# Half-block products in a two-layer decoder trunk: block sums kept in three half-size buffers and loaded three columns ahead

## The chip, the cores and the metric

The kernel runs on one core of a Trainium2 chip. The metric is the device time of one execution in microseconds (us). The profile uses short names for the engines: PE (matrix multiplication, with its weight loads shown as PEld), DVE (the vector engine), ACT (the scalar engine), POOL (the general engine, which here also issues DMAs) and SP (which only issues DMAs).

## What is computed

Two layers work on 512 positions of width 1024. The first mixes positions with a convolution module, the second with sparse attention, and each is followed by the same feed-forward network:

```python
def swiglu_ffn(h, w_in, w_out):
    gate, up = jnp.split(h @ w_in, 2, axis=-1)
    return (jax.nn.silu(gate) * up) @ w_out

for i in range(DEPTH):
    h = rmsnorm(x, norm_mix[i])
    x = x + mixer_i(h)
    h = rmsnorm(x, norm_ffn[i])
    x = x + swiglu_ffn(h, ffn_w_in[i], ffn_w_out[i])
```

The hidden width is 2816, which is 22 columns of 128. Only the products with `w_in` of 17 of these 22 columns, in both layers, are touched by the change.

## The kernel before

Data stand transposed: 128 features lie on the partitions, 512 positions along the rows. The products with the large weights are made exact enough by splitting each operand into a rounded high part and a low remainder. ACT writes the high part, DVE subtracts it from the original to get the low part, and PE adds up three products: high by high, high by low, low by high.

The feed-forward function `ffn` (line 636) makes the first five hidden columns (`NREG`) with ordinary products, two output tiles for each (gate and up). The other 17 (`NST`) are made by `pair` (line 791), once for each column. A column's weights are seen as four blocks of 512 elements: gate and up, each with a first and a second half of the inner dimension. The activations are seen as four blocks too (two halves of the inner dimension, two halves of the 512 positions, `H` = 256 each). With sums and differences of the blocks, seven products are enough instead of eight. So a column takes seven calls of `product` (line 759), each of twelve matmuls with a 128x256 moving operand: 84 matmuls.

The activation side is prepared once for each layer: `operand(c)` (line 695) is called for the four pieces of the inner dimension while the ordinary columns are still computed. DVE scales the input into `z`, POOL makes the differences `t1` to `t4`, and ACT and DVE split everything into `bh` and `bl`.

The weight side is prepared anew for each column n, in these steps:

- `s_load(n)`: SP loads one weight block into `raw[n]` (two buffers).
- `s_pre(n)`: POOL issues a DMA that puts two weight blocks into blocks 0 and 2 of the tile `S[n]` (four blocks of 512, two buffers).
- `s_acc(n)`: POOL issues an accumulating DMA, which adds a third block to both of them in place.
- `s_add(n)`: POOL adds the gate weights, which are the tile `wr`, to make block 1 from block 0 (line 741) and block 3 from block 1 (line 742).
- `s_g1(n)` and `s_g2(n)`: `s_part` splits blocks 0 and 1 into the parts `ga`, and blocks 2 and 3 into the parts `gb`. ACT copies 1024 elements (line 748), then DVE subtracts 1024 elements (line 749). The parts of `raw[n]` are `gc`. Each of these part tiles has one buffer, so the parts of column n+1 wait until PE has read those of column n.

Within `pair(n)` PE's order is written out by hand. I number its products:

- P0 uses the gate tile's own split `w1`, which `w_hi` (ACT, line 191) and `w_lo` (DVE, line 200) make ahead. The trace has them right behind P4 of an earlier pair.
- P1 uses the first half of `ga`.
- P2 (in `tail`) uses `gc` of the column before and ends that column.
- P3 uses the second half of `ga`.
- P4 uses `w1` again.
- P5 uses the second half of `gb`.
- P6 uses the first half of `gb`.

Small steps on ACT and DVE pick up the results: `copied` makes `c1`, `c5` and `c2` on ACT (line 770), DVE adds the two halves of `g` (lines 821 and 825), ACT applies silu to `g` (line 826), `t22` adds on DVE (line 789), and `post` multiplies on DVE (lines 782 and 783). P2 cannot begin before `t22` of the column before, because both touch the same bank.

Nearly all of these instructions carry `keep_in_program_order` (written `pe`), so each engine runs them in the order of the program text. For POOL this gives, in pair n: both adds of column n+1, the DMA issue of `s_pre(n+2)`, and then the DMA issue of `s_acc(n+2)`. An engine waits in place: whatever stands behind a waiting instruction on POOL waits too. `w_hi`, `w_lo` and the loads of `wr` are not pinned; the compiler's scheduler may move them.

Before the first pair the loop over the ordinary columns issues, at its fourth `operand`: two `s_load`, then on POOL `s_pre(0)`, `s_acc(0)`, `s_pre(1)`, `s_add(0)`, `s_acc(1)`.

Of the kernel before, what the change touches and what calls it, by code (L numbers as in the profile page):

```python
# [10 lines left out]
F32 = mybir.dt.float32  # L11
F32R = mybir.dt.float32r
BF16 = mybir.dt.bfloat16
I32 = mybir.dt.int32
AF = mybir.ActivationFunctionType
ALU = mybir.AluOpType
# [3 lines left out]
P = 128  # L20
T = 512
# [66 lines left out]
NST = NF - NREG  # L88
NB = 7
# [17 lines left out]
def trunk(ctx: ExitStack, tc: tile.TileContext, A, out):  # L107
    nc = tc.nc
# [8 lines left out]
    def nm(s):  # L117
        cnt[0] += 1
        return f"{s}_{cnt[0]}"
# [32 lines left out]
    for z in QV_ORDER:  # L152
        if z < 8:
            add("nw_q", z, 1024)
        else:
            w = VW[z - 8]
# [46 lines left out]
    def next_w(ahead=True):  # L203

        i = state["next"]
        w_hi(i)
        w_lo(i)
        state["next"] += 1
        if ahead and i + 1 < state["end"]:
            w_hi(i + 1)  # L210
        for k in range(i, min(i + 4, state["end"])):
            w_dma(k)
        return split[i]
# [25 lines left out]
    def v(col, n=1):  # L239
        return vec[:, col:col + n]  # L240
# [395 lines left out]
    def ffn(acc, gnext, layer):  # L636
# [7 lines left out]
        H = T // 2  # L644
        pe = tc.keep_in_program_order
        with ExitStack() as cx:
# [6 lines left out]
            sw = sx.enter_context(tc.tile_pool(name="sw", bufs=1, side="right", reuse_waits="tile"))  # L653
# [39 lines left out]
            bh, bl = [], []  # L693

            def operand(c):
                z = sw.tile([P, 4 * T], F32, tag="S", bufs=2, name=nm("z"))
                for i in range(2):
                    nc.vector.scalar_tensor_tensor(z[:, i * T:(i + 1) * T], x[c + 4 * i], v(gcol + c + 4 * i), R,
                                                   ALU.mult, ALU.mult)
                b11, b12, b21, b22, t1, t2, t3, t4 = (z[:, i * H:(i + 1) * H] for i in range(8))  # L700
                gp = nc.gpsimd
                gp.tensor_tensor(t1, b11, b12, ALU.subtract)
                gp.tensor_tensor(t3, b22, b12, ALU.subtract)
                gp.tensor_tensor(t2, t1, b22, ALU.add)
                gp.tensor_tensor(t4, t2, b21, ALU.subtract)
                gp.tensor_scalar(t2, t2, -1.0, None, ALU.mult)
                h_ = sb.tile([P, NB * H], F32R, tag=f"bh{c}", name=nm("bh"))
                l_ = sb.tile([P, NB * H], F32R, tag=f"bl{c}", name=nm("bl"))
                for d, e in ((slice(0, H), slice(0, H)), (slice(H, NB * H), slice(2 * H, 8 * H))):
                    nc.scalar.activation(h_[:, d], z[:, e], AF.Copy)  # L710
                    nc.vector.tensor_tensor(l_[:, d], z[:, e], h_[:, d], ALU.subtract)
                bh.append(h_)
                bl.append(l_)


            W, S, raw, part = {}, {}, {}, {}

            def s_load(n):
                if n >= NST:
                    return  # L720
                W[n] = A["fw_x"][layer * NST + n]
                raw[n] = sw.tile([P, T], F32, tag="r22", bufs=2, name=nm("r22"))
                nc.sync.dma_start(raw[n], W[n][:, :T])

            def odd(n):
                return S[n].rearrange("p (a c b) -> p a c b", a=2, c=2)[:, :, 0]

            def s_pre(n):
                if n >= NST:
                    return  # L730
                S[n] = sw.tile([P, 4 * T], F32, tag="S", bufs=2, name=nm("S"))
                pe(nc.gpsimd.dma_start(odd(n), W[n][:, :2 * T].rearrange("p (a b) -> p a b", a=2)))  # L732

            def s_acc(n):
                if n < NST:
                    pe(nc.gpsimd.dma_start(odd(n), W[n][:, None, 2 * T:].to_broadcast([P, 2, T]), accum_op=ALU.add))

            def s_add(n):
                if n < NST:
                    w = raws[u0 + n]  # L740
                    pe(nc.gpsimd.tensor_tensor(S[n][:, T:2 * T], S[n][:, :T], w[:, :T], ALU.add))  # L741
                    pe(nc.gpsimd.tensor_tensor(S[n][:, 3 * T:], S[n][:, T:2 * T], w[:, T:2 * T], ALU.add))  # L742

            def s_part(n, key, of, cols):

                h_ = sw.tile([P, cols], F32R, tag=key + "h", name=nm("sh"))
                l_ = sw.tile([P, cols], F32R, tag=key + "l", name=nm("sl"))
                pe(nc.scalar.activation(h_, of, AF.Copy))  # L748
                pe(nc.vector.tensor_tensor(l_, of, h_, ALU.subtract))  # L749
                part[n, key] = (h_, l_)  # L750

            def s_g1(n):
                if n < NST:
                    s_part(n, "ga", S[n][:, :2 * T], 2 * T)

            def s_g2(n):
                s_part(n, "gb", S[n][:, 2 * T:], 2 * T)

            def product(ps, w, i, b, first, last):
                wh, wl = w  # L760
                for c in range(4):
                    k = slice(i * T + c * P, i * T + (c + 1) * P)
                    t = slice(b * H, (b + 1) * H)
                    for q, (p_, m_) in enumerate(((wh, bh), (wh, bl), (wl, bh))):
                        pe(nc.tensor.matmul(ps[:, :H], p_[:, k], m_[c][:, t], start=first and c == 0 and q == 0,  # L765
                                            stop=last and c == 3 and q == 2, skip_group_check=True))

            def copied(ps, tag):
                t = ft.tile([P, H], F32, tag=tag, name=nm(tag))
                pe(nc.scalar.activation(t, ps[:, :H], AF.Copy))  # L770
                return t

            def bank():
                return pm.tile([P, T], F32, tag="pm", name=nm("st"))
# [9 lines left out]

                return post

            def t22(q):
                q["t"] = ft.tile([P, H], F32, tag="t22", name=nm("t22"))
                pe(nc.vector.tensor_tensor(q["t"], q["a"][:, :H], q["c5"], ALU.add))

            def pair(n, prev):
                q = dict(n=n, a=bank())
                last = n == NST - 1
                w1 = next_w(False)
                product(q["a"], w1, 0, 0, True, True)
                if prev:
                    t22(prev)
                s_g2(n)
                s_add(n + 1)
                s_load(n + 2)  # L800
                s_pre(n + 2)
                q["d"] = bank()
                product(q["d"], part[n, "ga"], 0, 3, True, True)
                c1 = copied(q["a"], "c1")
                post = tail(prev) if prev else None
                q["c5"] = copied(q["d"], "c5")
                if post:
                    post()
                w_hi(state["next"])
                w_lo()  # L810
                product(q["a"], part[n, "ga"], 1, 4, False, True)
                s_part(n, "gc", raw[n], T)
                b = bank()
                product(b, w1, 1, 1, True, True)
                c2 = copied(q["a"], "c2")
                s_g1(n + 1)
                if last:
                    product(q["a"], part[n, "gb"], 0, 5, False, True)
                product(q["d"], part[n, "gb"], 1, 2, False, True)
                g = q["g"] = ft.tile([P, T], F32, tag="g", name=nm("g"))  # L820
                pe(nc.vector.tensor_tensor(g[:, :H], b[:, :H], c1, ALU.add))
                s_acc(n + 2)
                if not last:
                    product(q["a"], part[n, "gb"], 0, 5, False, True)
                pe(nc.vector.tensor_tensor(g[:, H:], q["d"][:, :H], c2, ALU.add))
                pe(nc.scalar.activation(g, g, AF.Silu))
                return q

            act(0, pss[0], pss[1])
# [2 lines left out]
            for f in range(2, NREG):  # L832
                mids = []
                for z in range(2):
                    mids.append(proj_tile(pm, "pm"))
                    i = 2 * (f - 2) + z
                    if i < 4:
                        operand(i)
                    if i == 3:
                        s_load(0)  # L840
                        s_load(1)
                        s_pre(0)
                        s_acc(0)
                        s_pre(1)
                        s_add(0)
                        s_acc(1)
                act(f, *mids)
            hx[0].close()
            yx = ExitStack()
# [4 lines left out]
            q = None  # L854
            for n in range(NST):
                q = pair(n, q)
            t22(q)
            tail(q)()
            sx.close()
            fo = cx.enter_context(tc.tile_pool(name="fo", bufs=1, side="right", reuse_waits="tile"))  # L860
# [1 line left out]
            for m in range(NK):  # L862
                ps = pm.tile([P, T], F32, tag="pm", name=nm("fo"))
                for b, n in ((0, 8), (8, 8), (16, 6)):
                    wh, wl = next_w()
                    for k in range(n):
                        c = slice(k * P, (k + 1) * P)
# [11 lines left out]
                else:  # L879
                    n = OUT_N if m == NK - 1 else T  # L880
# [846 lines left out]
```

## Time and profile before

| what | value |
|---|---|
| time, median of 3 runs | 1408.66 us (1407.66 to 1409.84) |
| time of the profiled execution | 1403.82 us |
| its span in the trace | 1401.8 us |
| mean granted clock of PE | 0.962 |
| PE busy | 1280.7 us (91%), 8015 matmuls |
| DVE busy | 769.2 us (55%) |
| ACT busy | 561.8 us (40%) |
| POOL busy | 385.5 us (27%) |

The span runs from the first to the last instruction that the profiler saw; the execution's own time is 2 us longer. Busy shares are means over stages that differ much. PE's busy time also grows when its clock is low, because each matmul then takes longer, so a high share does not say that PE does useful work all the time. The chain of work that ended last names, step by step backwards, what released each piece of work; it is the view that tells which engine or transfer sets the time in a stage.

### The profile page before, as it was taken

Reading aid. Unit: us, or ns where it says so; the run is one execution under the profiler, and the core shown is the slowest. Engines: PE = TensorE matmul, PEld = TensorE weight load, DVE = VectorE, ACT = ScalarE, POOL = GpSimd, SP = SyncE. Lnnn points to the kernel's source line nnn. Section 1 sums busy time; section 2 is a strip of 40 time slices with the busy share of each in tenths; the row PEclk is TensorE's granted clock in tenths of the full one; section 3 lists DMA queues with packets and bytes.
Section 4 is the critical chain, followed back from the end, with each engine's and each line's share of the span. In section 5 each row is a group of like instructions: output and inputs, shape, how many; then the busy total and the mean of one; then the engine's idle time right before and its main releaser. Section 6 shows DMA issues by size and latency. Waiting matters only on the chain.

```text
span 1401.8 us, 20567 instructions
## 1 busy us (share of the span) xinstructions
PE 1280.7 (91%) x8015; PEld 1073.5 (77%) x8015; DVE 769.2 (55%) x1355; ACT 561.8 (40%) x970; POOL 385.5 (27%) x435
## 2 busy tenths in 40 slices
PE   8999899978887899999998999999998888879998
PEld 6887687877886878888777766668777788777887
DVE  6993778544443462335687787634763444346222
ACT  5222544433343342223453677743443434334111
POOL 2011036332323201131332556522543333230000
PEclk9999999999899899999999999999999899989999
DMA  8668232554454412344255010003255554541331
GB/s 322 216 228 242 60 114 76 158 140 118 129 136 118 125 59 92 98 118 118 91 137 146 17 46 9 16 31 106 84 149 128 136 128 136 128 124 64 110 105 57
DMA packets 82114, 161.61 MB, mean 115 GB/s; under 512 B 36064, under 2 KB 36960, under 8 KB 80480
## 3 DMA queue, kind: packets, MB, share of 16 engines
q1 hardware_dynamic: 65808, 108.54, 25.4%
q0 software_dynamic: 16208, 51.75, 14.2%
q8 instruction: 63, 1.03, 0.3%
q14 instruction: 35, 0.29, 0.1%
HBM read 146.73 MB, written 5.28 MB: 108 GB/s over the span
## 4 chain that ended last, share of the span: by engine, by line
PE 47%; DMA 18%; issue 13%; POOL 10%; DVE 9%; ACT 2%; SPq 2%; DVEq 0%; POOLq 0%; ACTq 0%
DMA S<-fw_x 16%; PE fo L253 6%; PE fo L252 6%; PE fo L251 6%; PE pp L253 5%; PE pp L251 5%; PE pp L252 5%; POOL S L741 3%; PE O L1468 3%; POOL S L742 3%; PE cpe L462 2%; PE st L765 2%; POOL S L732 2%; PE pv L1303 1%; DVE Pm L1414 1%
## 5 line engine op out<-in xcount | busy, mean ns | idle before, releaser
L200 DVE TENSOR_TENSOR wl<-wr,wh 128x1024 fp32r<-128x1024 f32 (+3 forms) x158 | 189.5, 1200 | 200.3 <-ACT wh L191 193.0
L191 ACT ACTIVATE wh<-wr 128x1024 fp32r<-128x1024 f32 (+3 forms) x158 | 160.4, 1015 | 328.5 <-PE fo L252 145.0
L765 PE MATMUL st<-bh,sh 128*128 128x256 f32 x680 | 213.9, 315 | 53.7 <-ACT sh L748 48.8
L765 PE MATMUL st<-bh,sl 128*128 128x256 f32 x680 | 212.8, 313 | 27.0 <-DVE sl L749 27.0
L765 PE MATMUL st<-bl,sh 128*128 128x256 f32 x680 | 208.5, 307 | 0.0
L765 PEld LDWEIGHTS st<-bh,sh 128*128 128x128 f32 x680 | 147.1, 216 | 62.2 <-ACT sh L748 55.0
L749 DVE TENSOR_TENSOR sl<-S,sh 128x1024 fp32r<-128x1024 f32 x68 | 85.8, 1264 | 188.4 <-ACT sh L748 188.4
L765 PEld LDWEIGHTS st<-bh,sl 128*128 128x128 f32 x680 | 147.6, 217 | 34.2 <-DVE sl L749 34.2
L253 PE MATMUL pp<-hh,wl 128*128 128x512 f32 x416 | 164.8, 399 | 3.9 <-DVE wl L200 3.9
L251 PE MATMUL pp<-hh,wh 128*128 128x512 f32 x416 | 165.3, 400 | 2.9 <-DVE gr L409 1.9
L252 PE MATMUL pp<-hl,wh 128*128 128x512 f32 x416 | 165.3, 398 | 0.1
L765 PEld LDWEIGHTS st<-bl,sh 128*128 128x128 f32 x680 | 147.6, 217 | 0.1
L252 PE MATMUL fo<-al,wh 128*128 128x512 f32 x352 | 139.8, 397 | 2.6 <-DVE al L670 2.6
L253 PE MATMUL fo<-ah,wl 128*128 128x512 f32 x352 | 139.4, 397 | 1.5 <-DVE wl L200 1.5
L251 PE MATMUL fo<-ah,wh 128*128 128x512 f32 x352 | 139.8, 397 | 1.0 <-ACT wh L191 1.0
L748 ACT ACTIVATE sh<-S 128x1024 fp32r<-128x1024 f32 x68 | 71.4, 1050 | 143.3 <-POOL S L741 142.7
L253 PEld LDWEIGHTS pp<-hh,wl 128*128 128x128 f32 x416 | 78.5, 189 | 24.4 <-DVE wl L200 6.4
L1429 POOL TENSOR_SCALAR Pm<-Pm,sm,gates 128x512 f32<-128x512 f32 (+3 forms) x128 | 79.8, 636 | 62.9 <-DVE sm L1425 50.1
L251 PEld LDWEIGHTS pp<-hh,wh 128*128 128x128 f32 x416 | 78.6, 189 | 24.2 <-ACT wh L191 2.5
L252 PEld LDWEIGHTS pp<-hl,wh 128*128 128x128 f32 x416 | 78.8, 189 | 19.3 <-issue 1.1
L741 POOL TENSOR_TENSOR S<-S,wr 128x512 f32<-128x512 f32 x34 | 43.6, 1283 | 175.1 <-DMA S<-fw_x 175.1
L295 POOL TENSOR_TENSOR acc<-acc,sq 128x512 f32<-128x512 f32 x18 | 31.6, 1754 | 207.9 <-ACT sq L293 194.1
(280 smaller groups left out, 2528.6 us busy)
## 6 DMA issues: line engine op xcount, KB each, us to landing
S<-fw_x POOLq DMA_DIRECT2D x68, 512.0 KB, 5.7
wr<-fw_in SPq DMA_DIRECT2D x46, 512.0 KB
wr<-fw_o SPq DMA_DIRECT2D x32, 512.0 KB
bd<-bands POOLq DMA_DIRECT2D x12, 1280.0 KB, 11.5
r<-fw_x SPq DMA_DIRECT2D x34, 256.0 KB
wr<-cw_in SPq DMA_DIRECT2D x14, 512.0 KB
wr<-fw_o SPq DMA_DIRECT2D x16, 384.0 KB
wr<-fw_s SPq DMA_DIRECT2D x8, 512.0 KB
```

The source lines that it names most:

```text
L191: after(nc.scalar.activation(hi[:, :cols], raws[i][:, :cols], AF.Copy), pin.get(AF))
L200: after(nc.vector.tensor_tensor(lo[:, :cols], raws[i][:, :cols], hi[:, :cols], ALU.subtract), pin.get(ALU))
L251: nc.tensor.matmul(ps, wh, xh, start=first, stop=False)
L252: nc.tensor.matmul(ps, wh, xl, start=False, stop=False)
L253: nc.tensor.matmul(ps, wl, xh, start=False, stop=last)
L741: pe(nc.gpsimd.tensor_tensor(S[n][:, T:2 * T], S[n][:, :T], w[:, :T], ALU.add))
L742: pe(nc.gpsimd.tensor_tensor(S[n][:, 3 * T:], S[n][:, T:2 * T], w[:, T:2 * T], ALU.add))
L748: pe(nc.scalar.activation(h_, of, AF.Copy))
L749: pe(nc.vector.tensor_tensor(l_, of, h_, ALU.subtract))
L765: pe(nc.tensor.matmul(ps[:, :H], p_[:, k], m_[c][:, t], start=first and c == 0 and q == 0, stop=last and c == 3 and q == 2, skip_group_che ...
L1429: nc.gpsimd.tensor_scalar(Pt, Pt, sm[:, k:k + 1], gates[:, t + k, br * 16 + h:br * 16 + h + 1], ALU.mult, ALU.mult)
L1468: pe(nc.tensor.matmul(o[par * 64:par * 64 + 64, P * kc:], vf[br][:, kc, g], Us[par][kc], start=False, stop=last))
```

## The change

The tile of sums is cut in two. `S[n]` now holds only the two blocks that the DMAs write (`s_pre` and `s_acc`), in three buffers of half the size. The two blocks that POOL adds go to a new tile `S2[n]`, which has one buffer.

The order of POOL's work changes. In pair n POOL now does the adds of column n+1, the issue of `s_acc(n+2)` and the issue of `s_pre(n+3)`. Before, it did the adds of n+1, the issue of `s_pre(n+2)` and, further down, the issue of `s_acc(n+2)`. Ahead of the first pair it is `s_pre(0)`, `s_pre(1)`, `s_acc(0)`, `s_acc(1)`, `s_add(0)`, `s_pre(2)`.

Since the four blocks are no longer neighbours, each split of 1024 elements becomes two of 512, on ACT and on DVE. The same buffers serve `operand`, which now takes two half-size tiles (`z` and `zt`) and splits in three pieces instead of two. Silu moves from the end of `pair(n)` to `finish` behind the first product of pair n+1; on ACT it still follows the parts `ga` of n+1 and precedes the parts `gb` of n+1.

```diff
             def operand(c):
-                z = sw.tile([P, 4 * T], F32, tag="S", bufs=2, name=nm("z"))
+                z, zt = (sw.tile([P, 2 * T], F32, tag="S", bufs=3, name=nm("z")) for _ in range(2))
...
-                for d, e in ((slice(0, H), slice(0, H)), (slice(H, NB * H), slice(2 * H, 8 * H))):
-                    nc.scalar.activation(h_[:, d], z[:, e], AF.Copy)
-                    nc.vector.tensor_tensor(l_[:, d], z[:, e], h_[:, d], ALU.subtract)
+                for d, e in ((slice(0, H), b11), (slice(H, 3 * H), z[:, T:]), (slice(3 * H, NB * H), zt)):
+                    nc.scalar.activation(h_[:, d], e, AF.Copy)
+                    nc.vector.tensor_tensor(l_[:, d], e, h_[:, d], ALU.subtract)
...
             def s_pre(n):
-                S[n] = sw.tile([P, 4 * T], F32, tag="S", bufs=2, name=nm("S"))
-                pe(nc.gpsimd.dma_start(odd(n), W[n][:, :2 * T].rearrange("p (a b) -> p a b", a=2)))
+                if n < NST:
+                    S[n] = sw.tile([P, 2 * T], F32, tag="S", bufs=3, name=nm("S"))
+                    pe(nc.gpsimd.dma_start(S[n], fw_x(n)[:, :2 * T]))
...
             def s_add(n):
                 if n < NST:
                     w = raws[u0 + n]
-                    pe(nc.gpsimd.tensor_tensor(S[n][:, T:2 * T], S[n][:, :T], w[:, :T], ALU.add))
-                    pe(nc.gpsimd.tensor_tensor(S[n][:, 3 * T:], S[n][:, T:2 * T], w[:, T:2 * T], ALU.add))
+                    t = S2[n] = sw.tile([P, 2 * T], F32, tag="S2", name=nm("S2"))
+                    pe(nc.gpsimd.tensor_tensor(t[:, :T], S[n][:, :T], w[:, :T], ALU.add))
+                    pe(nc.gpsimd.tensor_tensor(t[:, T:], t[:, :T], w[:, T:2 * T], ALU.add))
...
+                for i, z in enumerate(of):
+                    c = slice(i * T, (i + 1) * T)
+                    pe(nc.scalar.activation(h_[:, c], z, AF.Copy))
+                    pe(nc.vector.tensor_tensor(l_[:, c], z, h_[:, c], ALU.subtract))
...
             def s_g1(n):
                 if n < NST:
-                    s_part(n, "ga", S[n][:, :2 * T], 2 * T)
+                    s_part(n, "ga", S[n][:, :T], S2[n][:, :T])
 
             def s_g2(n):
-                s_part(n, "gb", S[n][:, 2 * T:], 2 * T)
+                s_part(n, "gb", S[n][:, T:], S2[n][:, T:])
...
-            def t22(q):
+            def finish(q):
+                pe(nc.scalar.activation(q["g"], q["g"], AF.Silu))
                 q["t"] = ft.tile([P, H], F32, tag="t22", name=nm("t22"))
...
                 if prev:
-                    t22(prev)
+                    finish(prev)
                 s_g2(n)
                 s_add(n + 1)
+                s_acc(n + 2)
                 s_load(n + 2)
-                s_pre(n + 2)
+                s_pre(n + 3)
...
-                s_acc(n + 2)
                 if not last:
                     product(q["a"], part[n, "gb"], 0, 5, False, True)
                 pe(nc.vector.tensor_tensor(g[:, H:], q["d"][:, :H], c2, ALU.add))
-                pe(nc.scalar.activation(g, g, AF.Silu))
...
                         s_pre(0)
+                        s_pre(1)
                         s_acc(0)
-                        s_pre(1)
+                        s_acc(1)
                         s_add(0)
-                        s_acc(1)
+                        s_pre(2)
```

More of the change, by code (lines that the diff above doesn't have):

```diff
@@ L699, in operand @@
                                                    ALU.mult, ALU.mult)
-                b11, b12, b21, b22, t1, t2, t3, t4 = (z[:, i * H:(i + 1) * H] for i in range(8))
+                b11, b12, b21, b22 = (z[:, i * H:(i + 1) * H] for i in range(4))
+                t1, t2, t3, t4 = (zt[:, i * H:(i + 1) * H] for i in range(4))
                 gp = nc.gpsimd
@@ L708, in operand, with fw_x @@
                 l_ = sb.tile([P, NB * H], F32R, tag=f"bl{c}", name=nm("bl"))
-                for d, e in ((slice(0, H), slice(0, H)), (slice(H, NB * H), slice(2 * H, 8 * H))):
-                    nc.scalar.activation(h_[:, d], z[:, e], AF.Copy)
-                    nc.vector.tensor_tensor(l_[:, d], z[:, e], h_[:, d], ALU.subtract)
+                for d, e in ((slice(0, H), b11), (slice(H, 3 * H), z[:, T:]), (slice(3 * H, NB * H), zt)):
+                    nc.scalar.activation(h_[:, d], e, AF.Copy)
+                    nc.vector.tensor_tensor(l_[:, d], e, h_[:, d], ALU.subtract)
                 bh.append(h_)
                 bl.append(l_)
-            W, S, raw, part = {}, {}, {}, {}
+            S, S2, raw, part = {}, {}, {}, {}
+            def fw_x(n):
+                return A["fw_x"][layer * NST + n]
             def s_load(n):
[L719 to L726, printed above, removed]
+                if n < NST:
+                    raw[n] = sw.tile([P, T], F32, tag="r22", bufs=2, name=nm("r22"))
+                    nc.sync.dma_start(raw[n], fw_x(n)[:, :T])
             def s_pre(n):
-                if n >= NST:
-                    return
-                S[n] = sw.tile([P, 4 * T], F32, tag="S", bufs=2, name=nm("S"))
-                pe(nc.gpsimd.dma_start(odd(n), W[n][:, :2 * T].rearrange("p (a b) -> p a b", a=2)))
+                if n < NST:
+                    S[n] = sw.tile([P, 2 * T], F32, tag="S", bufs=3, name=nm("S"))
+                    pe(nc.gpsimd.dma_start(S[n], fw_x(n)[:, :2 * T]))
             def s_acc(n):
                 if n < NST:
-                    pe(nc.gpsimd.dma_start(odd(n), W[n][:, None, 2 * T:].to_broadcast([P, 2, T]), accum_op=ALU.add))
+                    pe(nc.gpsimd.dma_start(S[n].rearrange("p (a b) -> p a b", a=2),
+                                           fw_x(n)[:, None, 2 * T:].to_broadcast([P, 2, T]), accum_op=ALU.add))
             def s_add(n):
@@ L740, in s_add, with s_part @@
                     w = raws[u0 + n]
[L741 to L749, printed above, removed]
+                    t = S2[n] = sw.tile([P, 2 * T], F32, tag="S2", name=nm("S2"))
+                    pe(nc.gpsimd.tensor_tensor(t[:, :T], S[n][:, :T], w[:, :T], ALU.add))
+                    pe(nc.gpsimd.tensor_tensor(t[:, T:], t[:, :T], w[:, T:2 * T], ALU.add))
+            def s_part(n, key, *of):
+                h_ = sw.tile([P, len(of) * T], F32R, tag=key + "h", name=nm("sh"))
+                l_ = sw.tile([P, len(of) * T], F32R, tag=key + "l", name=nm("sl"))
+                for i, z in enumerate(of):
+                    c = slice(i * T, (i + 1) * T)
+                    pe(nc.scalar.activation(h_[:, c], z, AF.Copy))
+                    pe(nc.vector.tensor_tensor(l_[:, c], z, h_[:, c], ALU.subtract))
                 part[n, key] = (h_, l_)
@@ L811, in pair @@
                 product(q["a"], part[n, "ga"], 1, 4, False, True)
-                s_part(n, "gc", raw[n], T)
+                s_part(n, "gc", raw[n])
                 b = bank()
@@ L856, in ffn @@
                 q = pair(n, q)
-            t22(q)
+            finish(q)
             tail(q)()
```

## The prediction

> **What bounds the kernel now.** I first read the page's chain of work that ended last, then PE's busy time and granted clock by stage, then that chain inside the first layer's 17 pairs.
>
> ```profile
> DMA S<-fw_x 16%; PE fo L253 6%; PE fo L252 6%; PE fo L251 6%; PE pp L253 5%; PE pp L251 5%; PE pp L252 5%; POOL S L741 3%; PE O L1468 3%; POOL S L742 3%; PE cpe L462 2%; PE st L765 2%; POOL S L732 2%; PE pv L1303 1%; DVE Pm L1414 1%
> ```
> ```profile
> 258.00:500.00 242.00, 201.14 (x1443) 192.30 (x1441) 104.89 (x155) 91.97 (x141) 71.97 (x65) 0.90 0.49 126
> 500.00:600.00 100.00, 97.67 (x415) 77.97 (x416) 40.84 (x52) 33.48 (x48) 9.00 (x5) 1.00 0.28 87
> ```
> ```profile
> by line: DMA S<-fw_x 44.8%; issue 32.5%; POOL S L741 8.6%; POOL S L742 7.8%; POOL S L732 4.7%; DVE y L688 0.5%; DVE wl L200 0.5%; DVE bl L711 0.4%; DVE g L684 0.3%; DVE y L687 0.3%; POOLq L741 0.1%; POOLq L732 0.0%; DVEq L200 0.0%
> ...
> 346.10 6.13 DMA S<-fw_x
> ...
> 352.31 1.29 POOL S L741
> ...
> 353.67 1.27 POOL S L742
> 354.94 0.69 POOL S L732
> 355.63 4.53 issue
> ...
> 360.18 5.89 DMA S<-fw_x
> ```
>
> In the pairs' stage (the window 258 to 500; columns: length, then busy time of PE, PEld, DVE, ACT and POOL, then the clock, the DMA share, GB/s) PE is granted 0.90 of its clock, against 1.00 in the stage behind it. The chain there holds no PE at all. It is a ring on POOL and its DMAs: the accumulating DMA lands 6.1 us after its start, the two adds take 1.29 and 1.27, the next load is issued, 5.2 us pass until it has landed (0.69 and the 4.53 that the view calls "issue", in which POOL waits for the load), and the next accumulating DMA starts. One turn, 346.10 to 360.18, is 14.1 us and makes one column. PE takes part as a victim:
>
> ```profile
> 259.51 0.28 PE L765 MATMUL st<-bh,wh 128*128 128x256 f32 x1
> ...
> 262.39 0.39 PE L765 MATMUL st<-bh,sl 128*128 128x256 f32 x1 [1.07 <-DVE sl L749]
> ...
> 340.56 0.58 PE L765 MATMUL st<-bh,sh 128*128 128x256 f32 x1 [3.28 <-ACT sh L748]
> ...
> 342.71 0.41 PE L765 MATMUL st<-bh,sl 128*128 128x256 f32 x1
> ...
> 489.99 0.28 PE L765 MATMUL st<-bh,sl 128*128 128x256 f32 x1
> ...
> 491.19 0.28 PE L765 MATMUL st<-bh,wh 128*128 128x256 f32 x1
> ...
> 492.60 0.40 PE L251 MATMUL fo<-ah,wh 128*128 128x512 f32 x1
> ...
> 494.00 0.28 PE L765 MATMUL st<-bh,sh 128*128 128x256 f32 x1
> ...
> 497.88 0.38 PE L765 MATMUL st<-bh,sh 128*128 128x256 f32 x1 [0.85 <-DVE t L789]
> ...
> 499.41 0.40 PE L251 MATMUL fo<-ah,wh 128*128 128x512 f32 x1
> ```
> ```profile
> 1032.25 0.28 PE L765 MATMUL st<-bh,wh 128*128 128x256 f32 x1
> ...
> 1272.03 0.40 PE L251 MATMUL fo<-ah,wh 128*128 128x512 f32 x1
> ```
>
> It idles 3.28 us for the split sums (340.56), and behind such a gap a matmul takes 0.41 us where it takes 0.28 in an undisturbed stretch. The stage runs from the first `st` matmul to the first matmul behind it: 239.9 us in layer 0 (259.51 to 499.41) and 239.8 in layer 1 (1032.25 to 1272.03).
>
> **What PE alone needs.** The counts and durations of the stage's groups:
>
> ```profile
> L765 PE MATMUL st<-bh,sh 128*128 128x256 f32 x340 | 106.9, 314 | 27.9 <-ACT sh L748 25.4 <-DVE t L789 2.4
> ...
> L749 DVE TENSOR_TENSOR sl<-S,sh 128x1024 fp32r<-128x1024 f32 x34 | 42.9, 1264 | 94.0 <-ACT sh L748 94.0
> ...
> L765 PE MATMUL st<-bh,wh 128*128 128x256 f32 x136 | 38.1, 280 | 0.0
> ...
> L200 DVE TENSOR_TENSOR wl<-wr,wh 128x1024 fp32r<-128x1024 f32 x18 | 22.0, 1220 | 26.6 <-ACT wh L191 26.6
> ...
> L191 ACT ACTIVATE wh<-wr 128x1024 fp32r<-128x1024 f32 x18 | 19.0, 1054 | 9.6 <-PE st L765 9.6
> L770 ACT ACTIVATE c<-st 128x256 f32<-128x256 f32 x51 | 18.1, 375 | 19.3 <-PE st L765 19.1
> L749 DVE TENSOR_TENSOR sl<-r,sh 128x512 fp32r<-128x512 f32 x17 | 11.6, 683 | 0.0
> ...
> L748 ACT ACTIVATE sh<-r 128x512 fp32r<-128x512 f32 x17 | 10.7, 630 | 15.1 <-PE st L765 9.9 <-issue 3.1 <-ACT c L770 2.0
> L826 ACT ACTIVATE g<-g 128x512 f32<-128x512 f32 x17 | 10.7, 630 | 37.2 <-DVE g L825 37.2
> ...
> L789 DVE TENSOR_TENSOR t<-st,c 128x256 f32<-128x256 f32 x17 | 6.9, 407 | 0.0
> ```
>
> Each form with the sums comes 340 times and there are three (20 of each in a pair, 60 together); each form with `w1` 136 times (8, 24 together). Ten sum matmuls take 1.20 us (489.99 to 491.19), twelve with `w1` 1.41 (491.19 to 492.60). A pair without a wait is 60 x 0.120 + 24 x 0.1175 = 10.02 us, and 17 pairs 170.3 us.
>
> **The change, part by part.** *The ring is opened.* With three buffers the load of n+3 and the accumulating DMA of n+2 are issued back to back, one behind the other, and each has a whole pair to land. The 5.2 us for the load leave the ring. What is left on POOL is the adds of n+1, then the accumulating DMA of n+2, then the adds of n+2. For that DMA's landing and for what may lengthen the adds:
>
> ```profile
> DMA to landing us min/median/max: 5.6/6.1/8.3
> ```
> ```profile
> L295 POOL TENSOR_TENSOR acc<-acc,sq x18: 1292/1792/1985, 176.4 to 969.3; 128x512 f32<-128x512 f32 x18
> ```
> ```profile
> L286 DVE SCALAR_TENSOR_TENSOR hl<-x,vec,hh x32: 740/745/1780, 4.8 to 974.7; 128x512 fp32r<-128x512 f32 x32
> ```
>
> The ring becomes 2.6 + 6.1 = 8.7 us, shorter than 10.02; PE sets the pace. The adds now run beside a busy DVE. Line 295 is a POOL add of the same shape in a place where DVE works: it takes up to 1.99 us against 1.29 undisturbed. So the adds cost 2.6 to 4.0 and the ring 8.7 to 10.1 at the median landing. I take 3.0, since only some DVE instructions fall beside them.
>
> The Trainium skill, page "SBUF — State Buffer", section "Who interferes with whom", has a rule against this change: a DVE instruction with two SBUF inputs and a POOL instruction that reads SBUF cannot run together, and the later one waits for the whole of the earlier. The two rows above agree (POOL 1.29 grows to 1.99, DVE 0.74 to 1.78). By it an unlucky pair holds one add for `wl` (1.22) and one for a half split (0.68), and the ring is 10.6; without it, 8.7.
>
> *What is late next.* I lay one pair out with t=0 at P0: P1 starts at 1.41, P2 2.85, P3 4.29, P4 5.73, P5 7.14, P6 8.58. ACT's `wh` ends at 8.2 and DVE's `wl` at 9.4. The halves of `ga` of n+1 follow: ACT to 9.5, DVE to 10.8, which is 0.8 in the next pair. There DVE's two `g` adds end at 1.6 and `t22` at 2.0; P2 wants it at 2.85. ACT's silu ends at 2.25, the halves of `gb` at 3.5, `c1` at 3.9; P3 overwrites its bank from 4.29. DVE ends `gb` at 4.3. Only then is the one `S2` buffer free: adds 4.3 to 7.3, accumulating DMA from 7.3, landed at 13.4, 3.4 in the next pair, where it is wanted at 4.3. `S2`'s first half is ready near 5.9 and wanted at 8.8. So every wait ends before PE needs it, by 0.4 to 3 us. Behind the waiting adds on POOL stand only the two DMA issues, for which there is a pair's time. SP's `wr` load waits for the adds as before, its `raw` load for `gc`.
>
> *Halved splits.* Two halves of 0.683 for 1.264 on DVE and two of 0.630 for about 1.05 on ACT: +0.1 and +0.2 for each part, twice a pair. Both hide in the layout above; uncovered they would lie on the way to `t22`, at most 0.3 a pair. *Silu*: its place on ACT is unchanged, cost 0.
>
> *What remains.* The tightest places are 0.4 (`c1`) and 0.85 (`t22`). If a held DVE instruction (1.78 - 0.74 = 1.04 us) hits them in one pair of seven, that is 0.15 a pair, 2.5 a layer; bounds 0 and 1.04 a pair (the latter needs a hit every time). The start wait of 1.07, the end wait of 0.85 and the six output matmuls inside the stage (492.60 to 494.00, 1.4) stay.
>
> *The start.* POOL's adds of column 0 move behind the issue of the second accumulating DMA:
>
> ```profile
> 250.93 1.25 POOL L736 DMA_DIRECT2D S<-fw_x  x1 [3.61 <-DMA S<-fw_x]
> 251.71 1.23 POOL L732 DMA_DIRECT2D S<-fw_x  x1
> 256.89 1.29 POOL L741 TENSOR_TENSOR S<-S,wr 128x512 f32<-128x512 f32 x1 [3.95 <-DMA S<-fw_x]
> ...
> 259.92 1.21 POOL L736 DMA_DIRECT2D S<-fw_x  x1 [0.39 <-issue]
> ```
>
> The second load now goes ahead of 250.93, lands about 5.2 later (251.71 to 256.89 is the nearest bound), and the second accumulating DMA's issue of 1.2 still fits before 256.89. I take 0, bounds 0 and 1.2 a layer. `operand` has three half tiles where it had the room of four; POOL's differences may wait for a free one or start sooner, since a half is freed sooner. I take 0, bounds -2 and +2 a layer (a pair of `z` writes, or two POOL differences).
>
> *The sum.* A layer's stage becomes 170.3 + 1.1 + 0.9 + 1.4 + 2.5 = 176.2; the savings are 63.7 and 63.6, together 127.3. The profiled execution took 1403.82, which would become 1276.5. It lies 4.8 below the median 1408.66, so I add 4.8: **1281 us**.
>
> **Rivals.** *The ring on POOL still sets the pace* (adds held, and the landing longer because `wr`, `raw`, the load and the accumulating DMA now start close together). For it: L295's 1.79 median and landings up to 8.3. Against it: the ring has 1.3 us to spare and `S2` 3 us more. At adds of 4.0 and a landing of 7.0 it is 11.0; (11.0 - 10.02) x 16 - 3 = 12.7 a layer, 1306 us. The lock of the Trainium skill's page "SBUF — State Buffer" would at its worst (10.6) give 1294.
>
> *The two POOL DMAs are served one after the other, so the overlap does not come*: 6.1 + 5.3 + 2.6 = 14.0, as now, 1408 us. Against it: before, the second load was issued 0.8 behind an accumulating DMA, and had landed by 259.92, where the next accumulation on its tile starts, 9.0 behind the first; one after the other would be 11.4.
>
> *Slower, by crowded DMAs*: it decides where a landing passes 14.1 - 2.6 = 11.5 us; at twice the median (12.2) a pair is 14.8, 34 x 0.7 = 24 us more, 1433. Against it: a DMA share of 0.49 over 14.1 us is 6.9 us of work a pair, 0.69 of 10.0.
>
> **How the numbers follow.** PE sets the pace: 0.75. The ring on POOL: 0.19. One after the other: 0.03. Crowded: 0.03. Low end: no held instruction (-5), both `operand` gains (-4) and part of the 4.8 between execution and median gone: 1268. High end: most of the ring's case, with 1.2 a layer at the start and 2 for `operand`: 1312. Beyond lie 0.03 + 0.03 and the tails. A difference under 0.2% cannot be told from none. Faster 0.94, same 0.03, slower 0.03.
>
> **What would show it.** Right: PE's clock near 1.00 in the pairs, one pair near 10.1 us, no matmul of 0.41 there, and a chain through PE's `st` instead of `S<-fw_x`. Wrong: POOL still idle for the DMA before each add with PE waiting for `sh` (the ring), `t22` or `c1` before PE's gaps each time (the hold), or loads that land only after the accumulating DMA.

## The result and the profile after

| | before | after |
|---|---|---|
| median of 4 runs each | 1408.16 us (1404.54 to 1409.84) | 1304.82 us (1300.98 to 1307.39) |
| profiled execution / span | 1403.82 / 1401.8 us | 1304.57 / 1302.8 us |
| granted clock of PE, mean | 0.962 | 0.995 |

The ratio is 0.9267, with a 95% interval from 0.9238 to 0.9297. The change makes the kernel 7.3% faster. That lies inside the range of the prediction, but it is 24 us above its forecast (1281, "PE sets the pace") and within 1.5 us of the time worked out for the rival "the ring on POOL still sets the pace" (1306). So the direction and most of the size were right, and the question is which of the two mechanisms runs on the chip.

First the page after: the chain of work that ended last.

```profile
PE st L767 12%; PE pp L253 7%; PE pp L251 7%; PE pp L252 7%; PE fo L253 6%; PE fo L252 6%; PE fo L251 6%; PE O L1471 3%; DVE wl L200 3%; DVE sl L751 2%; POOL S L741 2%; PE cpe L462 2%; PE T L1445 1%; DVE Pm L1417 1%; ACT sh L750 1%
```

The transfer `S<-fw_x`, which led the chain of before with 16%, is gone from it, and PE's `st` matmuls now lead. Now the stage of the pairs itself, as windows from the first `st` matmul to the first matmul behind the stage, in layer 0 and layer 1 (columns: bounds, length, busy time of PE, PEld, DVE, ACT and POOL, clock, DMA share, GB/s):

```profile
260.30:450.79 190.49, 178.51 (x1435) 172.82 (x1434) 129.29 (x188) 93.02 (x174) 76.13 (x64) 1.00 0.62 157
985.34:1172.93 187.59, 177.89 (x1435) 172.64 (x1434) 128.02 (x188) 91.04 (x170) 72.87 (x61) 1.00 0.62 158
```

The granted clock is 1.00 in both, where it was 0.90 in the window of before. Layer 0's stage fell from 239.90 to 190.49 us, layer 1's from 239.78 to 187.59: 101.6 us together, where the prediction had 127.3. The first `st` matmul comes 0.8 us later than before (259.51 to 260.30), and the stretch between the two stages is 1.7 us longer (499.41 to 1032.25, 532.84 us, against 450.79 to 985.34, 534.55). These 2.5 us and the 14.3 and 11.4 us by which the two stages miss their 176.2 are the whole difference between the 1276.5 forecast for the profiled execution and its 1304.57.

What paces a pair now stands in the timeline of POOL (columns: start, duration, engine and line, operation; in brackets the idle time before it and what ended it):

```profile
278.21 1.30 POOL L741 TENSOR_TENSOR S<-S,wr 128x512 f32<-128x512 f32 x1 [7.01 <-DVE sl L751]
...
333.00 1.30 POOL L741 TENSOR_TENSOR S<-S,wr 128x512 f32<-128x512 f32 x1 [6.70 <-issue]
334.38 1.63 POOL L742 TENSOR_TENSOR S<-S,wr 128x512 f32<-128x512 f32 x1
335.94 1.21 POOL L734 DMA_DIRECT2D S<-fw_x  x1
336.70 1.04 POOL L730 DMA_DIRECT2D S<-fw_x  x1
344.76 1.29 POOL L741 TENSOR_TENSOR S<-S,wr 128x512 f32<-128x512 f32 x1 [7.02 <-issue]
...
433.57 1.28 POOL L741 TENSOR_TENSOR S<-S,wr 128x512 f32<-128x512 f32 x1 [7.12 <-issue]
```

One turn here is 333.00 to 344.76, 11.76 us; over the fourteen turns from 278.21 to 433.57 the mean is 11.10, which is 1.08 more than the 10.02 that PE needs. A turn consists of the two adds (2.94 from the first's start to the issue of the accumulating DMA, line 734) and of that DMA's landing. (The "issue" in the brackets says only that the profile names no releaser for POOL; that it is the landing is read from ACT below. Of the 17 adds of layer 0, 12 are marked so and four wait for DVE's `sl`, as the one at 278.21 does: a second loop, which comes up in the experiments.) The source view of line 734 gives the landings, first between 275 and 385 us and then in the whole run:

```profile
DMA to landing us min/median/max: 6.7/8.1/8.7
```
```profile
DMA to landing us min/median/max: 6.5/8.2/9.5
```

That is the ring, with the load of line 730 no longer in it, and with a landing two microseconds longer than the 6.1 of before. How PE meets it is seen in the timelines of ACT, DVE and PE ahead of one P2, and in PE's waits in layer 0 (line, releaser: us in total, times, longest):

```profile
332.98 0.63 ACT L750 ACTIVATE sh<-S 128x512 fp32r<-128x512 f32 x1 [1.78 <-DMA S<-fw_x]
```
```profile
333.64 2.92 DVE L751 TENSOR_TENSOR sl<-S,sh 128x512 fp32r<-128x512 f32 x2 [2.88 <-ACT sh L750]
336.49 0.41 DVE L825 TENSOR_TENSOR g<-st,c 128x256 f32<-128x256 f32 x1
336.82 1.21 DVE L200 TENSOR_TENSOR wl<-wr,wh 128x1024 fp32r<-128x1024 f32 x1
337.95 0.41 DVE L828 TENSOR_TENSOR g<-st,c 128x256 f32<-128x256 f32 x1
338.29 0.41 DVE L792 TENSOR_TENSOR t<-st,c 128x256 f32<-128x256 f32 x1
```
```profile
338.75 0.39 PE L767 MATMUL st<-bh,sh 128*128 128x256 f32 x1 [0.90 <-DVE t L792]
```
```profile
PE st L767 <- DVE t L792: 9.9, 12, 1.2
```

ACT and POOL both start at 333.0, when the DMA lands. DVE's two half splits run beside the two adds and take 2.92 us from the first's start to the second's end, where two halves undisturbed take 1.3 (1.29 a little later, at 339.64); `g`, `wl`, `g` and `t22` stand behind them, and PE gets `t22` 0.90 us late. Read alone, the wait says "`t22` is the bound". That gave two theories. **Theory 1**: the ring sets the pace, its landing being longer because the gate weights `wr`, the next load and the raw block are now under way at the same time. **Theory 2**: POOL's adds hold DVE, so that `t22` is late in each pair whatever the landing is.

### The profile page after: what moved, and what is told of

Same layout as the page of the kernel before. It is cut to its first block, busy times and chain, and to the rows that moved or that the text cites. A ratio compares the mean times of both kernels' runs of the same rounds, so it can differ in the third digit from the quotient of the medians.

```text
span 1302.8 us, 20773 instructions
## 1 busy us (share of the span) xinstructions
PE 1239.0 (95%) x8015; PEld 1035.7 (80%) x8015; DVE 821.6 (63%) x1431; ACT 566.6 (43%) x1046; POOL 394.5 (30%) x435
## 4 chain that ended last, share of the span: by engine, by line
PE 61%; DVE 17%; issue 9%; DMA 4%; POOL 4%; ACT 3%; SPq 2%; DVEq 0%; ACTq 0%; POOLq 0%
PE st L767 12%; PE pp L253 7%; PE pp L251 7%; PE pp L252 7%; PE fo L253 6%; PE fo L252 6%; PE fo L251 6%; PE O L1471 3%; DVE wl L200 3%; DVE sl L751 2%; POOL S L741 2%; PE cpe L462 2%; PE T L1445 1%; DVE Pm L1417 1%; ACT sh L750 1%
## 5 line engine op out<-in xcount | busy, mean ns | idle before, releaser
L767 PE MATMUL st<-bh,sh 128*128 128x256 f32 x680 | 197.9, 291 | 19.5 <-DVE t L792 19.0
L751 DVE TENSOR_TENSOR sl<-S,sh 128x512 fp32r<-128x512 f32 x136 | 135.1, 1018 | 106.8 <-ACT sh L750 103.3
L767 PE MATMUL st<-bh,sl 128*128 128x256 f32 x680 | 192.3, 283 | 2.1 <-DVE sl L751 2.1
L767 PE MATMUL st<-bl,sh 128*128 128x256 f32 x680 | 191.9, 282 | 0.0
L767 PEld LDWEIGHTS st<-bh,sh 128*128 128x128 f32 x680 | 129.5, 190 | 29.6 <-DVE t L792 23.8
L767 PEld LDWEIGHTS st<-bh,sl 128*128 128x128 f32 x680 | 129.9, 191 | 2.5 <-DVE sl L751 2.5
L767 PEld LDWEIGHTS st<-bl,sh 128*128 128x128 f32 x680 | 130.3, 192 | 0.1
L750 ACT ACTIVATE sh<-S 128x512 fp32r<-128x512 f32 x136 | 81.5, 624 | 67.3 <-DMA S<-fw_x 42.6
L741 POOL TENSOR_TENSOR S<-S,wr 128x512 f32<-128x512 f32 x34 | 46.5, 1367 | 207.9 <-issue 156.9
```

The costliest lines, as they stand in the source:

```text
L741: pe(nc.gpsimd.tensor_tensor(t[:, :T], S[n][:, :T], w[:, :T], ALU.add))
L750: pe(nc.scalar.activation(h_[:, c], z, AF.Copy))
L751: pe(nc.vector.tensor_tensor(l_[:, c], z, h_[:, c], ALU.subtract))
```

## The experiments

All kernels were timed in three rounds against the kernel before; the ratios are to it, with 95% intervals, and the differences to the changed kernel are between medians (those worked out from the ratios agree within 2 us). The first four kernels ran on one chip, the last four on another.

**Gate weights not loaded (no_wr).** In `w_dma`:

```diff
+        k = i - state.get("u0", i)
+        if 3 <= k < 14:
+            raws[i] = raws[state["u0"] + 1 + k % 2]
+            return
```

> Leaves out the loads of the gate weights of columns 3 to 13 in both layers (22 loads of 512 KB); those columns use the gate weights of columns 1 and 2 in their place, all other work stays. Theory 1 (the ring on POOL sets the pace, and the landing of the accumulating DMA grew from 6.1 to 8.3 us because the gate weights, the next load and the raw block are under way with it): in those pairs the landing falls to 6.5 to 7, the ring from 11.1 to about 9.7, PE sets the pace at 10.1; 22 pairs x 1.0 = 22 us less, about 1283. Theory 2 (POOL's adds hold DVE's low parts of ga by the shared port, and PE waits for t22 behind them, whatever the landing is): no change, 1302 to 1307.

Measured: 1276.77 us, ratio 0.9081 (0.9057 to 0.9104), 28 us below the changed kernel. The landing between 275 and 385 us, and the stage of layer 0:

```profile
DMA to landing us min/median/max: 6.5/7.0/8.8
```
```profile
258.17:433.86 175.69, 172.59 (x1435) 171.57 (x1434) 122.62 (x188) 93.20 (x174) 73.02 (x64) 1.00 0.56 138
```

The landing fell by 1.1 us and the stage to 175.69 us, the forecast's 176.2. The adds were made as before. The time is 6 us below theory 1's 1283. Theory 2 needs no gate weights and would have kept the time; it falls as it stands. This kernel leaves out the traffic itself, not only its place in time; `add_twice_off` and `acc_first` below keep every byte. The group of the first add (line 745 here) in that window shows the ring giving way: of POOL's idle time ahead of it, 46.1 us are put down to the DMA and 33.5 to DVE, whose parts of the column before free `S2`.

```profile
L745 POOL TENSOR_TENSOR S<-S,wr 128x512 f32<-128x512 f32 x17 | 23.3, 1371 | 93.0 <-DMA S<-fw_x 46.1 <-DVE sl L755 33.5 <-issue 6.8
```

**The second add repeated away from the ring (add_twice_off).** Behind `s_pre(n + 3)` in `pair`:

```diff
+                if n + 1 < NST:
+                    t, w = S2[n + 1], raws[u0 + n + 1]
+                    pe(nc.gpsimd.tensor_tensor(t[:, T:], t[:, :T], w[:, T:2 * T], ALU.add))
```

> The second add of each column is made once more behind the issue of the load, where POOL has some 6 us without work (the output stays the same). Theory 1 (the ring): the repeat lies outside the ring, 0 to 5 us more. Theory 2 (POOL's adds hold DVE): one more POOL instruction of 1.3 to 1.6 us beside DVE's wl, g and t22 in each of 32 pairs, 20 to 50 us more.

Measured: 1318.65 us, ratio 0.9367 (0.9345 to 0.939), 14 us above the changed kernel. Both theories miss. POOL's timeline and a row of DVE's say why:

```profile
346.52 1.29 POOL L741 TENSOR_TENSOR S<-S,wr 128x512 f32<-128x512 f32 x1 [5.62 <-DVE sl L751]
347.89 1.37 POOL L742 TENSOR_TENSOR S<-S,wr 128x512 f32<-128x512 f32 x1
349.20 1.17 POOL L734 DMA_DIRECT2D S<-fw_x  x1
349.95 1.01 POOL L730 DMA_DIRECT2D S<-fw_x  x1
350.55 1.74 POOL L808 TENSOR_TENSOR S<-S,wr 128x512 f32<-128x512 f32 x1
357.91 1.28 POOL L741 TENSOR_TENSOR S<-S,wr 128x512 f32<-128x512 f32 x1 [5.62 <-DVE sl L751]
```
```profile
349.73 3.73 DVE L751 TENSOR_TENSOR sl<-S,sh 128x512 fp32r<-128x512 f32 x2
```
```profile
DMA to landing us min/median/max: 6.3/6.7/6.9
```

The adds wait for DVE here, not for the DMA. A turn is 11.39 us (346.52 to 357.91), and its path runs through the one `S2` buffer: adds, DMA issues, the repeated add, which holds DVE's halves of `ga` (3.73 instead of 1.3), then the DVE work behind them, then the parts `gb` that free `S2`. So a second loop exists, and the repeat had made it the longer one. I called this **theory 3**: in the changed kernel too, the loop through `S2` is the bound or a close second. The landing is a by-product worth noting. SP issues the load of `wr` when the repeat has ended, 3.1 us behind the accumulating DMA (352.32 against 349.20), where in the changed kernel it follows 0.1 behind (336.04 against 335.94), and the landing is 6.7 us though no byte less is moved. SP's rows, first here and then in the changed kernel:

```profile
352.32 0.33 SPq L181 DMA_DIRECT2D wr<-fw_in  x1
```
```profile
336.04 0.33 SPq L181 DMA_DIRECT2D wr<-fw_in  x1
```

**The next load ahead of the adds (pre_first).** POOL's order becomes `s_pre(n+3)`, adds, `s_acc(n+2)`; one line of `pair` moves up. If the load beside it is what lengthens the landing, this shortens it.

> POOL issues the load of column n+3 ahead of the adds instead of behind the accumulating DMA. Theory 1 (the ring, its landing lengthened by the load that starts with it): the load starts some 4 us earlier, the landing falls to about 7.3, the ring to about 10.2, 1280 to 1290. If the load is no part of the lengthening (only the gate weights are): the ring stays 11, 1300 to 1310. Theory 2 (POOL's adds hold DVE): the adds stay where they are, 1300 to 1310.

Measured: 1310.31 us, ratio 0.9318 (0.9288 to 0.9348), 5 us above the changed kernel. The landing between 275 and 385 us did not fall:

```profile
DMA to landing us min/median/max: 7.3/8.1/8.7
```

In this order the load is issued 4.7 us behind one accumulating DMA and 6.4 ahead of the next (338.19, 342.87, 349.28), while `wr` still starts 0.1 us behind each. Taking the load away does not shorten the landing as long as `wr` starts with it.

**Halved splits and moved silu, in the kernel before (halves_alone).**

```diff
-                pe(nc.scalar.activation(h_, of, AF.Copy))
-                pe(nc.vector.tensor_tensor(l_, of, h_, ALU.subtract))
+                for i in range(0, cols, T):
+                    c = slice(i, i + T)
+                    pe(nc.scalar.activation(h_[:, c], of[:, c], AF.Copy))
+                    pe(nc.vector.tensor_tensor(l_[:, c], of[:, c], h_[:, c], ALU.subtract))
```

The line of silu also moves from the end of `pair` to the front of `t22`.

> The kernel before with two parts of the change alone: splits in halves of 512 and silu behind the first product of the next pair; buffers and POOL's order as before. The prediction took both at nothing. In the old order the parts ga stand on the path behind the adds: the second half's copy and subtraction come 0.1 and 0.2 us later, but the first half's low part comes 0.9 us earlier, which the first product of the sums needs. 0 to 0.3 us a pair less or more, 1398 to 1418.

Measured: 1420.24 us, ratio 1.0094 (1.0066 to 1.0123): slower than before by 13, above what was expected. POOL's adds and DVE's halves:

```profile
355.79 1.26 POOL L741 TENSOR_TENSOR S<-S,wr 128x512 f32<-128x512 f32 x1 [5.08 <-DMA S<-fw_x]
357.13 1.62 POOL L742 TENSOR_TENSOR S<-S,wr 128x512 f32<-128x512 f32 x1
```
```profile
356.46 1.15 DVE L751 TENSOR_TENSOR sl<-S,sh 128x512 fp32r<-128x512 f32 x1 [3.43 <-ACT sh L750]
...
357.75 1.55 DVE L751 TENSOR_TENSOR sl<-S,sh 128x512 fp32r<-128x512 f32 x1
```

With whole splits, DVE began only when the second add was nearly over (in the kernel before at 354.71, the add ending at 354.94). With halves its first half begins beside the first add (356.46, the add lasting from 355.79 to 357.05), is still running when the second add begins, and the second half runs beside that add. The second add takes 1.62 us where it took 1.27 (the median of 34, 1263 to 1297 ns, before). The old ring has this add in it: 0.35 x 34 is 12 us, close to the measured loss. It isn't spread evenly: in the profiled executions the stage of layer 0 is 4.3 us longer and that of layer 1 10.9 (244.22 and 250.69 us against 239.90 and 239.78), and the landing's median in layer 1 is 6.4 us where it was 6.1.

**Silu alone, in the kernel before (silu_alone).** Only that line moves.

> The kernel before with silu alone moved behind the first product of the next pair. ACT's order of instructions is the same: within 0.2%, 1404 to 1410. If the 13 us of the run with halves and silu were silu's: about 1420.

Measured: 1407.14 us, ratio 0.9991 (0.9963 to 1.0018). No difference, so the 13 us of the kernel above are the halves'.

**The second add made twice in its place (add_twice).** In `s_add` its line stands twice, ahead of the issue of the accumulating DMA.

> The second add of each column is made twice at its place, ahead of the issue of the accumulating DMA (same output). Theory 1 (the ring sets the pace): the ring grows by 1.4 to 1.7, 32 pairs, 45 to 55 us more, about 1353. If the ring were not the bound: what the same repeat cost behind the issue, 14 us, about 1319.

Measured: 1356.83 us, ratio 0.9631 (0.9599 to 0.9663), 52 us above the changed kernel. POOL's timeline, the add and its repeat (line 743), 1.61 us:

```profile
341.47 1.62 POOL L742 TENSOR_TENSOR S<-S,wr 128x512 f32<-128x512 f32 x1
343.17 1.61 POOL L743 TENSOR_TENSOR S<-S,wr 128x512 f32<-128x512 f32 x1
```

34 x 1.61 is 55 us. Nearly the whole of an added microsecond in that place comes out as time: the adds lie on the path that sets the pace. The same add behind the issues cost 14.

**Four buffers, issues further ahead (four).** Four half-size buffers; `s_pre(n+4)` and `s_acc(n+2)` stand so that a whole pair or more lies between each DMA and the work that needs it:

```diff
-                s_add(n + 1)
                 s_acc(n + 2)
-                s_load(n + 2)
-                s_pre(n + 3)
+                s_add(n + 1)
+                s_pre(n + 4)
```

To make room, `raw` has one buffer with its load behind the parts `gc`, `t22` writes over `c5`, and `c2` is written into `g`; there is one more `s_pre` at the start. One `S2` buffer stays.

> Four half-size buffers for S: the load runs four columns ahead and POOL issues the accumulating DMA of n+2 ahead of the adds of n+1, so its landing has more than a pair and no ring is left. The 4 KB a partition come from one raw buffer in place of two, c2 written into g, and t22 written over c5. Theory 1 (the ring with its crowded landing is all that keeps PE from its own pace): a pair near 10.1, the stage near 176, 1304.8 - 26 = 1276 to 1284. Theory 3 (a second loop stands close behind the ring: the one S2 buffer, the adds, DVE's low parts of ga, g, silu, gb; it gave 11.4 with the repeated add): its length without the repeat is the bound, 10.5 to 11, 1290 to 1305.

Measured: 1280.9 us, ratio 0.9084 (0.906 to 0.9108), 24 us below the changed kernel. Both stages, POOL's timeline, and the landing between 290 and 385 us:

```profile
261.87:435.68 173.81, 172.44 (x1435) 171.54 (x1434) 116.36 (x188) 92.08 (x170) 67.42 (x61) 1.00 0.68 172
977.75:1151.65 173.90, 172.52 (x1435) 171.55 (x1434) 116.46 (x188) 92.08 (x170) 67.18 (x60) 1.00 0.67 171
```
```profile
344.24 1.29 POOL L741 TENSOR_TENSOR S<-S,wr 128x512 f32<-128x512 f32 x1 [5.59 <-DVE sl L751]
...
346.84 0.59 POOL L730 DMA_DIRECT2D S<-fw_x  x1
347.42 1.23 POOL L734 DMA_DIRECT2D S<-fw_x  x1
354.25 1.30 POOL L741 TENSOR_TENSOR S<-S,wr 128x512 f32<-128x512 f32 x1 [5.60 <-DVE sl L751]
```
```profile
DMA to landing us min/median/max: 9.4/9.9/10.6
```

A pair is now 10.01 us (344.24 to 354.25), PE's own pace. The landing is the longest of all, 9.9 us right behind another load of the same queue, and it costs next to nothing: in the whole run two waits end on it, 3.3 and 0.2 us. The single `S2` buffer is there and does not lengthen the pair either, though 15 of the 17 adds of layer 0 wait for it: theory 3's loop is no longer than PE's pace unless an add is put into it.

**One line moved (acc_first).** The changed kernel, with `s_acc(n + 2)` ahead of `s_add(n + 1)`:

```diff
-                s_add(n + 1)
                 s_acc(n + 2)
+                s_add(n + 1)
```

> Three buffers as in the change; POOL issues the accumulating DMA of n+2 ahead of the adds of n+1. The adds no longer stand between one landing and the next issue, but the load of n+3 is issued only behind them, and the next accumulating DMA waits for it: a ring of load landing, issue and adds, 5.3 to 7 + 1.2 + 2.9 = 9.4 to 11.1. Theory 1: 1277 to 1305, by that landing. Theory 3: not under 1290.

Measured: 1281.67 us, ratio 0.9097 (0.9065 to 0.9128), as good as four buffers. Both stages, POOL's timeline, and DVE's half splits beside the adds:

```profile
259.46:437.58 178.12, 174.68 (x1435) 172.09 (x1434) 138.59 (x188) 91.89 (x174) 74.06 (x64) 1.00 0.64 168
973.62:1149.37 175.75, 173.73 (x1436) 171.84 (x1434) 135.69 (x188) 90.61 (x170) 70.48 (x61) 1.00 0.65 169
```
```profile
338.91 1.17 POOL L734 DMA_DIRECT2D S<-fw_x  x1 [6.31 <-DMA S<-fw_x]
339.64 1.75 POOL L741 TENSOR_TENSOR S<-S,wr 128x512 f32<-128x512 f32 x1
341.48 1.65 POOL L742 TENSOR_TENSOR S<-S,wr 128x512 f32<-128x512 f32 x1
343.07 0.61 POOL L730 DMA_DIRECT2D S<-fw_x  x1
348.16 1.18 POOL L734 DMA_DIRECT2D S<-fw_x  x1 [4.48 <-DMA S<-fw_x]
...
359.10 1.17 POOL L734 DMA_DIRECT2D S<-fw_x  x1 [6.18 <-DMA S<-fw_x]
```
```profile
339.82 3.86 DVE L751 TENSOR_TENSOR sl<-S,sh 128x512 fp32r<-128x512 f32 x2 [0.98 <-ACT sh L750]
```

The landing of the accumulating DMA has left the ring. Between 290 and 385 us it is back at the 6.1 of before, and `wr` starts only behind the adds (343.15, 4.2 us behind it):

```profile
DMA to landing us min/median/max: 5.6/6.1/7.2
```
```profile
343.15 0.33 SPq L181 DMA_DIRECT2D wr<-fw_in  x1
```

This also settles a rival of theory 1 that I had not named: the change gave the accumulating DMA another target (one stretch of `S` instead of two separate blocks), which might by itself have lengthened its landing. Here the target is the changed one and the landing is 6.1.

What POOL waits for is now the load: 343.07 to 348.16 is 5.1 us, and with the adds (3.4) and the issue of the DMA this turn is 9.25 us. The next is 10.94 (348.16 to 359.10), and over fourteen turns of layer 0 the mean is 9.92, hardly under PE's 10.02; this ring is a close second. So the kernel keeps the load that the change had taken out, and takes out the longer transfer instead. The stages are 4.3 and 1.9 us longer than those of `four`, which loses about as much outside them. The run is also the hardest on theory 2: the adds hold DVE's halves longer than in the changed kernel (3.86 against 2.92), yet PE's waits for `t22` in layer 0 come to 1.4 us instead of 9.9. Theory 3 (not under 1290) falls too. This and `four` beat both kernels.

## Why the prediction was right about the side and missed the size

- **"The 5.2 us for the load leave the ring": right.** POOL's rows after show the adds, the accumulating DMA and the wait for it, with the load's issue behind them and no wait for the load.
- **"The ring becomes 2.6 + 6.1 = 8.7 us" (8.7 to 10.1 with held adds), "shorter than 10.02; PE sets the pace": the step that failed.** The adds were sized well: 3.0 taken, 2.94 measured. The landing was not: I took 6.1, the median of a kernel in which `wr` starts 8.9 us behind it (346.10 in the prediction's rows; SP's row of before stands below), for a kernel that starts `wr` 0.1 us behind the accumulating DMA. It measured 8.2 over the whole run. 2.94 + 8.2 is 11.1 us, above PE's 10.02. Fourteen turns at 1.08 over it are 15 us; layer 0's stage missed by 14.3 beyond the 2.5 allowed for held instructions, 16.8 in all.

```profile
354.96 0.33 SPq L181 DMA_DIRECT2D wr<-fw_in  x1
```

- **The rival with the ring came true in mechanism; that its time did too is partly luck.** It named 4.0 for the adds and 7.0 for the landing, the sum 11.0 being right and both terms off by a microsecond in opposite directions. The measured time lies in the range because the range's high end was taken from this rival, not because the mechanism that I gave 0.75 held. The rival's reason, transfers starting close together, holds with a correction: leaving out `wr` shortens the landing (8.1 to 7.0), and starting `wr` 3.1 us later goes with 6.7, while moving the load away leaves 8.1. I gave it 0.19 by "1.3 us to spare", a margin that stood on the unchanged landing.
- **"A pair without a wait is 10.02 us": right.** In `four` it is 10.01.
- **Halved splits, "+0.1 and +0.2, both hide": wrong in its place.** I looked for their cost on ACT and DVE. It is on POOL: the first half now begins beside the first add and reaches into the second, which takes 0.35 us more, and the old ring lost 13 us. In the changed kernel this lies within the 3.0 taken for the adds; without it the ring would be about 10.7, an estimate (11.10 - 0.35).
- **The lock.** The Trainium skill's page "SBUF — State Buffer", section "Who interferes with whom", lets a DVE instruction with two SBUF inputs and a POOL instruction that reads SBUF run only one after the other. The rows bear out that they hold each other: two half splits 2.92 instead of 1.3, the add 1.62 instead of 1.27. They also fit waiting for the whole: in `halves_alone` the first half ends 0.56 us behind the first add (356.46 + 1.15 against 357.05) and the second 0.55 behind the second (357.75 + 1.55 against 357.13 + 1.62), where a half alone takes 0.69, and the second add, begun with some 0.5 us of the first half still to come, grew by 0.35. No run was made to test it. The 10.6 that I worked out by it came near the measured 11.1 only by chance: the adds stayed at the 3.0 taken, and the landing made the difference.
- **Silu 0: right** (ratio 0.9991). **The start and `operand`, 0 each:** 0.8 us at the start of layer 0, where the first add begins at 260.0 instead of 256.89, and 1.7 between the stages. Both lie inside the bounds and are read from the traces; no run took them apart.
- **`t22` and `c1`, the tight places:** PE does wait for `t22`, 9.9 us in layer 0. But with a shorter landing or another order the pair goes at PE's pace, or close to it, with the same adds, so `t22` was the place where the ring's lateness reached PE, not its cause. The layout also had `wl` end ahead of the halves of `ga`. In the trace after it stands between the two `g` adds (336.82), which puts its 1.21 us ahead of `t22`; `four` has it in the same place and keeps PE's pace.
- **The other rivals fell.** One after the other would have been a turn of 14.0, and crowding needed a landing over 11.5. A turn was 11.1, the longest landing 9.5.

Two things stay open. `add_twice_off` lost 14 us; the turn of 11.39 against 11.10 explains 10 of them (0.29 x 34). In the profiled executions, 15.3 us apart, the two stages are 11.4 us longer together, the stretch between them 3.3, and the start 0.7; why the stretch between is longer stays open. And `four`, whose stages are 14 to 17 us shorter than those of the changed kernel, had its first `st` matmul 1.6 us later in layer 0, and 542.07 us between its stages instead of 534.55; its profiled execution had a lower clock there (0.98) and was the longest of its four, so how much of this is the kernel's was not settled.

## What to carry to other kernels

When a wait is taken out of a ring, add up what is left with the landings that the new overlap will have, not with those of the old trace; a margin of 1.3 us on a landing of 6.1 was none. Where one engine both issues transfers and computes in program order, look for the order that takes the longest landing off the way from one issue to the next: moving one line here was worth 23 us, nearly as much as a fourth buffer. And a finer split can cost an engine that it does not touch, by starting earlier beside that engine's work (here 13 us).

## What the runs showed of the hardware

The landing of the same accumulating DMA, with the same bytes, had medians of 6.1, 6.7, 7.0, 8.1 and 9.9 us, depending on what was under way: 6.1 with the next load and `wr` both some 4.2 us behind it (`acc_first`; the 256 KB of `raw` start 0 to 3 us behind), 6.7 with the load 0.8 and `wr` 3.1 us behind (`add_twice_off`), 7.0 with the load 0.8 behind and most `wr` loads gone (`no_wr`), 8.1 with `wr` starting 0.1 behind (the changed kernel and `pre_first`), and 9.9 right behind a load of its own queue, with `wr` 0.8 behind (`four`). I had taken landings for a property of the transfer. Here they depended on its neighbours: another queue's load of 512 KB that starts with it went with 1.1 to 1.4 us more (8.1 against 7.0 and 6.7), and having that load start 3.1 us later was enough to lose it. What the transfers share was not measured.

A DVE subtraction of 512 elements that takes 0.69 us alone took 1.15 and 1.55 beside POOL's adds, and an add of 1.27 took 1.62 (`halves_alone`).
